# Two gate projections computed in the first stage of a hybrid layer and handed to the second through DRAM, with smaller pools for k, q and scores

## The chip, the cores and the metric

The kernel runs on one core of one Trainium2 chip. The metric is the device time of one execution in microseconds (us). A core has five engines with a queue each: the tensor engine (PE), the vector engine (DVE), the scalar engine (ACT), GpSimd (POOL) and the sync engine (SP), which here issues every transfer. An engine takes its queue strictly in the order in which it was written, so an instruction that waits holds back all behind it.

## The reference, cut to what matters

One layer over 4096 prompt tokens and 8 short sequences of 16 tokens (128 sample tokens), model width 1024:

```python
h = _rmsnorm(x, norm_w)
proj = h @ w_in                                   # one projection, split by columns
qkv, z_a, b_a, a_a, hq, hf, hi, z_b = jnp.split(proj, offs, axis=-1)
qkv_c, new_buf = _causal_conv(qkv, conv_buf, conv_w)
o_a, S_gdn_new = _gated_delta(q_a, k_a, v_a, g, beta, S_gdn, c)      # group A, 8 heads of 64
o_a = _rmsnorm(o_a, gdn_norm_w) * jax.nn.silu(z_a)
o_b, S_hg_new = _hgrn2(q_b, k_b, v_b, logf, S_hg, c)                 # group B, 4 heads of 128
o_b = _rmsnorm(o_b, hg_norm_w) * jax.nn.silu(z_b)
y = x + jnp.concatenate([o_a, o_b], -1) @ w_out   # then a final RMSNorm
```

`z_a` and `z_b` are the two gates, 512 columns each. They depend on x alone and are used only just before the output projection.

## The kernel before

The 33 tiles of 128 tokens form 17 groups: group 0 is the sample tile, groups 1 to 16 have two prompt tiles each. The work runs in two stages.

**Stage A** (`phase_a`) does group A for all groups and leaves its normed output in DRAM (`oa`) and the normed inputs, split in two fp16 parts, in DRAM (`xd`). For a group it projects q, k and v (`proj`: 12 blocks `acc` of 24 matmuls, each followed by ACT, POOL and DVE steps of the convolution, `u`, `c`, `c0`, written to `kq` and `vv`); makes the scores of both tiles (`gdn_pre`: matmuls `pk`, then DVE writes `WA`, lines 573 and 574); sends their diagonal blocks to DRAM (`wdr`) and reads them back spread over the partitions (`N`, line 623); inverts them on DVE by a chain of 62 dependent instructions `tm`, `X` (`gdn_inv`, lines 632 to 639); sends the inverse to DRAM and back (`xdr`, `tx`); transposes it (`tT`, line 656) and couples the blocks (`pv`, `V`, `px`, `tx`). Then the recurrence (`gdn_rec`) runs tile by tile: `pks`, `r`, `py`, `w`, `pcr`, `r`, `pz`, `w`, `pss`, the state `S` (line 737), the output `po`, its norm (`jo`, `no`) and `on` (line 769). The recurrence of a tile is the last reader of its `WA` and of its `kv`, that of a group's second tile the last reader of the group's `kq`.

A program loop with index g has, in this order, the recurrence of group g-1, the scores and the inverse of g, and the projections of g+1. Beside that `wspill` prepares the weights of stage B (`za`, `zb`, `hf`, `hq`, `hi` and the two halves of `w_out`, `o0`, `o1`) in small steps: it splits them in fp16 parts and writes them to DRAM.

**Stage B** (`phase_b`) does group B, gates, output projection and final norm. Per group: `hg_proj` (blocks `hac` of hq and hf), the score levels (`hg_levels`), `hg_tok` (projections `tphi`, `tpza`, `tpzb` of 24 matmuls with 512 columns per tile; the gate as (1 + tanh) times the projection, lines 1039 and 1040) and `hg_tile` (recurrence, norm, gate, output projection `py`, final norm, store). The weights of the gates and of `o0` come from DRAM into the slots in which stage A kept `WA` and `kv`, so they are loaded once A has ended.

Pools decide how far the groups overlap: `WA` and `kv` have 4 buffers (two groups of two tiles), `kq` 3.

The order on each engine is not written out. A scheduler in the framework lays out all instructions once, by the order of the program and its own estimate of the durations and of the free buffers, and each engine then follows that fixed list.

Of the kernel before, what the change touches and what calls it, by code (L numbers as in the profile page):

```python
# [16 lines left out]
P = 128  # L17
# [8 lines left out]
class Kern:  # L26
# [10 lines left out]
    # ---------------------------------------------------------------- consts  # L37
    def consts(self, ctx):
# [15 lines left out]
        # small vectors as rows, transposed on the tensor engine  # L54
# [15 lines left out]
        # conv taps times one half: [p, tap, block]  # L70
# [3 lines left out]
        # -2 exp(A_log), dt_bias on all partitions  # L74
# [7 lines left out]
    def masks(self):  # L82
# [3 lines left out]
        # mi[t, i] = t <= i  # L86
# [3 lines left out]
        # sequence of a token of the sample tile: sm[t, s], b16[t, i], ms[t, i] = b16 and t <= i  # L90
# [23 lines left out]
    def wprep(self, c0, c1, hi, lo, us, stg, eng):  # L114
        """hi + lo = (rows of w_in scaled by norm_w) * s in fp16 parts, us = 1 / (s * XS), s a power of two."""
# [15 lines left out]
    def wspill(self):  # L131
        """the same for the weights of phase B, to DRAM in fp16 parts, by steps of 128 columns"""
# [9 lines left out]
        def stage(nm, src, c):  # L142
            st = self.ex.tile([P, NDC, P], F32, tag="st", name=f"st{nm}{c}")
            with self.tc.issue_after(self.mark.ins):
                nc.sync.dma_start(st, src[:, :, c:c + P])
            nc.gpsimd.tensor_tensor(st, st, fac[nm][:, :, None].to_broadcast([P, NDC, P]), ALU.mult)
            return st

        for nm, src, c0 in names:
            fac[nm] = wrow if src is wout else self.nw  # L150
            self.wd[nm] = self.wdp.tile([P, 2, NDC, 512], F16, tag=f"wd{nm}", name=f"wd{nm}")
# [27 lines left out]
        for nm, src, c0 in names:  # L179
# [11 lines left out]

    def wa(self, name):
        return self.ex.tile([P, 2, 8, P], F32, tag="WA", name=name, bufs=4)
# [6 lines left out]
    # ---------------------------------------------------------------- phase A  # L200
    def shared(self, ctx):
        """what both phases use"""
# [4 lines left out]
        self.qp = pool("qp", 3)  # L207
# [8 lines left out]
    def phase_a(self, oa, xd):  # L216
        nc, tc, i, o = self.nc, self.tc, self.i, self.o
        with ExitStack() as ctx:
# [15 lines left out]
            def stage(g):  # L234
                if g < 4:
# [3 lines left out]
                return self.qp.tile([P, NDC, 256], F32, tag="kq", name="wst5")  # L239
# [7 lines left out]
            # last rows of the sample's convolution state, as columns  # L247
# [25 lines left out]
            # current tap, on the unscaled projection  # L273
# [8 lines left out]

            spill = self.wspill()
            nsp = -(-84 // max(ng - 1, 1))
            for g in range(-1, ng + 1):
# [60 lines left out]
    def xload(self, g, k, d):  # L346
        """x of a tile, normed, times XS"""
        nc = self.nc
        if k == 0:
# [7 lines left out]
        nc.scalar.activation(d["xl"][:, :, k * P:k * P + P], x.rearrange("p (c e) -> p c e", c=NDC), AF.Square,  # L357
                             accum_out=ss[:, 0:1])
        # XS * (mean + eps) ** -0.5
# [4 lines left out]
    def xtrans(self, g, k, d, xd):  # L364
        """its fp16 parts with the channels on the partitions"""
# [20 lines left out]
    def gate(self, g, d):  # L386
        """beta; decays: cumulative G, exp(total - G), G along the free axis in DRAM."""
# [24 lines left out]
        # softplus(y) = max(y, 0) + 2 atanh(e / (2 + e)), e = exp(-|y|)  # L412
# [44 lines left out]
    def mm3(self, out, wh, wl, xh, xl):  # L457
        """out = w^T x over the chunks, without the product of the low parts."""
# [7 lines left out]
    def proj(self, g, d):  # L466
# [7 lines left out]
        if samp:  # L474
            # states of the sequences [r k, s, p, v] for the head pairs p = 0, 1 and 2, 3
            Sn = [kq[:, 1].rearrange("p s (q v) -> p s q v", v=64),
                  self.wa("Sn1")[:, 0].rearrange("p h (a b) -> p h a b", a=2)]
# [39 lines left out]
    def gdn_pre(self, g, k, d):  # L517
# [16 lines left out]
        # exp(G) by channel; decay between tokens of the chunk, [j, h, i], zero for i < j  # L534
# [13 lines left out]
        # token layout of k, q, v  # L548
# [6 lines left out]
        kv = self.ex.tile([P, 2, 8, 64], F32, tag="kv", name=f"kv{nm}", bufs=4)  # L555
# [22 lines left out]
        # its value at the end of the chunk, or of the sequences  # L578
# [5 lines left out]
    def gdn_pre2(self, g, k, d):  # L584
# [10 lines left out]
        # 64 * eps * sum, for the norm of o  # L595
# [5 lines left out]
        # k, q times exp(G)  # L601
# [24 lines left out]
        # rows of the identity, those of one parity on one half of the partitions  # L626
# [13 lines left out]
        # to [j of 64, h, i of 64] by way of DRAM  # L640
# [33 lines left out]
    def gdn_rec(self, g, k, d, oa):  # L674
# [53 lines left out]
        # state  # L728
# [32 lines left out]
        # norm of the heads  # L761
# [11 lines left out]
    def b_begin(self, xd):  # L773
        """weights and first projections of phase B, in the place of those of phase A"""
        nc, w = self.nc, self.wp
        self.B = {}
# [25 lines left out]
        # za, zb, o0 go where A keeps what it needs of a tile  # L802
# [390 lines left out]
```

## Time and profile before

| | us |
|---|---|
| three timed runs | 2981.66, 2983.92, 2987.39 |
| median | 2983.92 |
| profiled execution, span from the first to the last instruction | 2983.5 |

| over the span | PE | DVE | ACT | POOL |
|---|---|---|---|---|
| busy us | 2598.1 | 1752.2 | 1219.2 | 991.0 |
| share | 87% | 59% | 41% | 33% |

The profiled execution's own time is its span, 2983.5 us; it lies 0.4 us from the median, so there is nothing to account for around the span. The shares are means over two stages that are limited differently: stage A lasts to about 1540 us, stage B from there to the end, with some overlap. Busy time of PE counts each matmul from its start to its modelled end, and successive matmuls overlap, so the distance between two starts says how fast PE works. A wait is put down to what ended last.

### The profile page before, as it was taken

Reading aid. Unit: us, or ns where it says so; the run is one execution under the profiler, and the core shown is the slowest. Engines: PE = TensorE matmul, PEld = TensorE weight load, DVE = VectorE, ACT = ScalarE, POOL = GpSimd, SP = SyncE. Lnnn points to the kernel's source line nnn. Section 1 sums busy time; section 2 is a strip of 40 time slices with the busy share of each in tenths; the row PEclk is TensorE's granted clock in tenths of the full one; section 3 lists DMA queues with packets and bytes.
Section 4 is the critical chain, followed back from the end, with each engine's and each line's share of the span. In section 5 each row is a group of like instructions: output and inputs, shape, how many; then the busy total and the mean of one; then the engine's idle time right before and its main releaser. Section 6 shows DMA issues by size and latency. Waiting matters only on the chain.

```text
span 2983.5 us, 67579 instructions
## 1 busy us (share of the span) xinstructions
PE 2598.1 (87%) x27628; PEld 1847.4 (62%) x27628; DVE 1752.2 (59%) x4215; ACT 1219.2 (41%) x3930; POOL 991.0 (33%) x1300
## 2 busy tenths in 40 slices
PE   4768678877877887778899999999999999999997
PEld 4656566665666666666674666666656666665664
DVE  7786778777778788876644434444433344433343
ACT  6656565555555665555332222222222222222222
POOL 5755565465565665655320001110001111000110
PEclk9888999888898989888999999999999999999999
DMA  6334232233343333333233231111110111111010
GB/s 180 100 100 122 68 107 74 73 101 106 98 121 77 96 103 99 97 94 115 77 92 112 73 98 40 43 51 44 51 47 24 46 44 50 44 51 34 32 37 33
DMA packets 298701, 227.78 MB, mean 76 GB/s; under 512 B 186409, under 2 KB 263614, under 8 KB 293782
## 3 DMA queue, kind: packets, MB, share of 16 engines
q1 hardware_dynamic: 298390, 223.45, 25.6%
q8 instruction: 217, 3.56, 0.5%
q14 instruction: 94, 0.77, 0.1%
HBM read 151.78 MB, written 71.62 MB: 75 GB/s over the span
## 4 chain that ended last, share of the span: by engine, by line
PE 49%; DVE 28%; DMA 13%; ACT 2%; issue 2%; POOL 2%; SPq 2%; DVEq 0%; POOLq 0%; ACTq 0%
DMA N<-wdr 7%; DVE X L638 6%; DVE c L510 5%; DVE tm L636 5%; PE py L1016 4%; PE py L1014 4%; PE py L1015 4%; PE hac L462 4%; PE hac L464 4%; PE hac L463 4%; PE sc L954 2%; PE tpzb L1014 2%; PE tpza L1014 2%; PE tpzb L1015 2%; PE tpzb L1016 2%
## 5 line engine op out<-in xcount | busy, mean ns | idle before, releaser
L462 PE MATMUL acc<-xt,w 128*128 128x256 f16 (+1 forms) x1632 | 468.9, 289 | 38.5 <-ACT c L504 36.8
L464 PE MATMUL acc<-xt,w 128*128 128x256 f16 (+1 forms) x1632 | 468.0, 288 | 2.7 <-DVE w L129 2.7
L463 PE MATMUL acc<-xt,w 128*128 128x256 f16 (+1 forms) x1632 | 468.9, 289 | 0.0
L510 DVE SCALAR_TENSOR_TENSOR c<-u,cw,c 128x256 f32<-128x256 f32 (+1 forms) x408 | 237.0, 584 | 31.0 <-POOL c L508 29.8
L1145 DVE SCALAR_TENSOR_TENSOR xr<-py,ysc,xr 128x512 f32<-128x512 f32 x66 | 49.5, 750 | 302.3 <-PE py L1016 302.3
L638 DVE TENSOR_TENSOR X<-X,tm 128x126 f32<-128x126 f32 (+26 forms) x527 | 220.5, 418 | 7.3
L512 ACT ACTIVATE c<-c 128x256 f32<-128x256 f32 (+1 forms) x204 | 83.4, 409 | 322.3 <-DVE c L510 197.6
L463 PEld LDWEIGHTS <-w 128*128 128x128 f16 x1632 | 171.9, 105 | 67.8 <-issue 41.3
L1014 PE MATMUL py<-wo,oh 128*128 128x512 f16 x528 | 201.0, 381 | 4.7 <-ACT oh L1137 3.5
L1016 PE MATMUL py<-wo,ol 128*128 128x512 f16 x528 | 201.1, 381 | 0.2
L1015 PE MATMUL py<-wo,oh 128*128 128x512 f16 x528 | 201.0, 381 | 0.0
L462 PEld LDWEIGHTS <-w 128*128 128x128 f16 x1632 | 172.2, 106 | 37.6 <-issue 9.9
L464 PEld LDWEIGHTS <-w 128*128 128x128 f16 x1632 | 172.0, 105 | 33.5 <-issue 3.3
L636 DVE TENSOR_TENSOR tm<-X,N 128x126 f32<-128x126 f32 (+26 forms) x527 | 187.9, 357 | 7.1
L1048 POOL TENSOR_TENSOR zs<-zs,pw_m 128x1 f32<-128x1 f32 x33 | 20.9, 632 | 469.6 <-DVE zs L1047 469.6
L508 POOL TENSOR_TENSOR c<-c,c 128x256 f32<-128x256 f32 (+1 forms) x204 | 155.9, 766 | 50.9 <-ACT c L507 41.8
L462 PE MATMUL hac<-bxt,whq 128*128 128x256 f16 (+1 forms) x544 | 147.4, 273 | 9.0 <-DVE q L924 9.0
L463 PE MATMUL hac<-bxt,whq 128*128 128x256 f16 (+1 forms) x544 | 147.2, 273 | 0.0
L464 PE MATMUL hac<-bxt,whq 128*128 128x256 f16 (+1 forms) x544 | 147.0, 273 | 0.0
L462 PE MATMUL hac<-bxt,whf 128*128 128x256 f16 (+1 forms) x544 | 145.4, 270 | 0.0
L464 PE MATMUL hac<-bxt,whf 128*128 128x256 f16 (+1 forms) x544 | 145.4, 270 | 0.0
L463 PE MATMUL hac<-bxt,whf 128*128 128x256 f16 (+1 forms) x544 | 145.3, 270 | 0.0
(399 smaller groups left out, 6692.3 us busy)
## 6 DMA issues: line engine op xcount, KB each, us to landing
E<-gdr SPq DMA_DIRECT2D x33, 512.0 KB
out_dram<-xr SPq DMA_DIRECT2D x33, 512.0 KB
x<-in_x_prompt_dram SPq DMA_DIRECT2D x32, 512.0 KB
xd<-xt SPq DMA_DIRECT2D x16, 1024.0 KB
bxt<-xd SPq DMA_DIRECT2D x16, 1024.0 KB
xr<-in_x_prompt_dram SPq DMA_DIRECT2D x32, 512.0 KB
tx<-xdr SPq DMA_DIRECT2D x66, 128.0 KB
oa<-on SPq DMA_DIRECT2D x33, 256.0 KB
```

Of the source, the lines that this page charges most:

```text
L462: nc.tensor.matmul(out, wh[k], xh[k], start=(k == 0), stop=False)
L463: nc.tensor.matmul(out, wh[k], xl[k], start=False, stop=False)
L464: nc.tensor.matmul(out, wl[k], xh[k], start=False, stop=(k == n - 1))
L508: nc.gpsimd.tensor_tensor(c, c, c0, ALU.add)
L510: nc.vector.scalar_tensor_tensor(cv, taps[j], self.cw[:, j, b:b + 1], cv, ALU.mult, ALU.add)
L512: nc.scalar.activation(th, c, AF.Tanh)
L636: nc.vector.tensor_tensor(tv, X[:, 0:R, m:m + 1].to_broadcast([2 * SY, R, c]), N[:, m:m + 1, m + 1:32].to_broadcast([2 * SY, R, c]), ALU.mult)
L638: nc.vector.tensor_tensor(X[:, 0:R, m + 1:32], X[:, 0:R, m + 1:32], tv, ALU.subtract)
L954: nc.tensor.matmul(ps[b:b + 32, k, h], KS[:, k, h, b:b + 32], rhs(k, h, slice(b, b + 32)), start=True, stop=True, tile_position=(0, b))
L1014: nc.tensor.matmul(acc, xh[:, dc], wh[dc], start=(dc == 0), stop=False)
L1015: nc.tensor.matmul(acc, xh[:, dc], wl[dc], start=False, stop=False)
L1016: nc.tensor.matmul(acc, xl[:, dc], wh[dc], start=False, stop=(dc == NDC - 1))
```

## The change

The gates are projected in stage A. `wspill` now prepares `za` and `zb` first and leaves them in on-chip memory. From group 3 on, `zproj` follows `proj` of the same group and writes the finished gate of a tile to DRAM (`zd`) in two halves; for the groups 0 to 2 (5 tiles) it comes after the last group's projections, on inputs that are loaded again (`zload`). Stage B loads the gate (`zg`, 512 KB a tile) in place of the projections. The weights `o0` and `o1` of stage B go where `za` and `zb` were. `WA` and `kv` go from 4 to 3 buffers and `kq` from 3 to 2, and some staging slots of the start change. The temporary `zt` shares the two slots `on` of the recurrence's output and of the weights' fp16 parts.

```diff
-        for nm, src, c0 in names:
+        for nm, src, c0 in names[:2]:
+            yield from sums(nm, src, c0)
+        for nm, src, c0 in names[:2]:
+            t = w.tile([P, 2, NDC, 512], F16, tag=f"w{nm}", name=f"w{nm}")
+            self.B[nm] = [[t[:, e, dc] for dc in range(NDC)] for e in range(2)]
+            for c in range(4):
+                st = stage(nm, src, c0 + c * P)
+                cc = slice(c * P, c * P + P)
+                nc.scalar.copy(t[:, 0, :, cc], st)
+                nc.gpsimd.tensor_tensor(t[:, 1, :, cc], st, t[:, 0, :, cc], ALU.subtract)
+                yield
...
+    def zproj(self, g, d):
+        nc = self.nc
+        for k, t in enumerate(self.groups[g]):
+            for n, name in enumerate(("za", "zb")):
+                acc = self.tokproj(name, d["xh"], d["xl"], k, f"{g}_{k}")
+                zt = self.tp.tile([P, 512], F32, tag="on", name=f"zt{g}_{k}_{n}")
+                nc.scalar.activation(zt, acc, AF.Tanh, scale=self.us5[name])
+                nc.vector.scalar_tensor_tensor(zt, zt, 1.0, acc, ALU.add, ALU.mult)
+                nc.sync.dma_start(self.zd[t][:, 512 * n:512 * n + 512], zt)
+    def zload(self, g, xd):
+        xt = self.xtp.tile([P, 2, NDC, 2 * P], F16, tag="xt", name=f"zxt{g}")
+        N = len(self.groups[g]) * P
+        nc = self.nc
+        if N == 2 * P:
+            nc.sync.dma_start(xt, xd[g])
+        else:
+            nc.sync.dma_start(xt[:, :, :, 0:N], xd[g][:, :, :, 0:N])
+        return {"xh": xt[:, 0, :, 0:N], "xl": xt[:, 1, :, 0:N]}
...
-        return self.ex.tile([P, 2, 8, P], F32, tag="WA", name=name, bufs=4)
+        return self.ex.tile([P, 2, 8, P], F32, tag="WA", name=name, bufs=3)
...
-        self.qp = pool("qp", 3)
+        self.qp = pool("qp", 2)
...
-            nsp = -(-84 // max(ng - 1, 1))
+            nsp = -(-60 // max(ng - 4, 1))
+            late = min(3, ng)
...
                     self.proj(g + 1, st[g + 1])
-                for _ in range(0 if g < 0 else nsp if g < ng - 2 else 99):
+                    if g + 1 >= late:
+                        self.zproj(g + 1, st[g + 1])
+                for _ in range((8, 4, 4)[g + 1] if g < 2 else nsp if g < ng - 2 else 99):
                     next(spill, None)
                 if g == ng - 1:
+                    for z in range(late):
+                        self.zproj(z, self.zload(z, xd))
...
-        kv = self.ex.tile([P, 2, 8, 64], F32, tag="kv", name=f"kv{nm}", bufs=4)
+        kv = self.ex.tile([P, 2, 8, 64], F32, tag="kv", name=f"kv{nm}", bufs=3)
...
-        for n, nm in enumerate(("hf", "hq", "hi")):
-            t = w.tile([P, 2, NDC, 512], F16, tag=f"w{n}", name=f"w{nm}")
+        for nm, tag in (("hf", "w0"), ("hq", "w1"), ("hi", "w2"), ("o0", "wza"), ("o1", "wzb")):
+            t = w.tile([P, 2, NDC, 512], F16, tag=tag, name=f"w{nm}")
...
+        zg2 = self.ex.tile([P, 2, 2, 512], F32, tag="WA", name=f"zg{g}", bufs=3)
         for k, t in enumerate(self.groups[g]):
             nm = f"{g}_{k}"
             v = vs[k]
-            if k == 0:
-                zg2 = self.qp.tile([P, 2, 2, 512], F32, tag="kq", name=f"zg{g}")
             zg = zg2[:, k]
-            for n, name in enumerate(("za", "zb")):
-                acc = self.tokproj(name, xh, xl, k, nm)
-                nc.scalar.activation(zg[:, n], acc, AF.Tanh, scale=self.us5[name])
-                nc.vector.scalar_tensor_tensor(zg[:, n], zg[:, n], 1.0, acc, ALU.add, ALU.mult)
-                if n == 0:
-                    yield
+            nc.sync.dma_start(zg, self.zd[t].rearrange("p (a b) -> p a b", a=2))
```

Since the scheduler orders the engines anew, the diff doesn't show where the work now stands. Three places follow. In these rows a name ends with the group, the tile of the group and a buffer number: `WA9_1_...` are the scores of the second tile of group 9. Line numbers are those of the kernel that the rows belong to; in the changed kernel the lines 616, 617, 699, 756, 766, 780, 812 and 675 are what 573, 574, 656, 713, 723, 737, 769 and 632 were.

DVE in the kernel before, from the transposed inverse of group 8 to the first step on the scores that were read back for group 9:

```order
L656 STREAM_TRANSPOSE tT8_0_10099<-tx8_0_10096 128x256
...
L574 TENSOR_TENSOR WA9_1_11094<-pk9_1_0_11095,E9_11014 128x2x2x128
L766 SCALAR_TENSOR_TENSOR no7_1_9890<-no7_1_9890,nrm7_8799 128x8
...
L769 TENSOR_TENSOR on7_1_9901<-po7_1_9817,no7_1_9890 128x512
L573 TENSOR_TENSOR WA9_1_11094<-pk9_1_1_11102,E9_11014 128x2x2x128
L574 TENSOR_TENSOR WA9_1_11094<-pk9_1_1_11102,E9_11014 128x2x2x128
...
L632 TENSOR_TENSOR N9_11121<-N9_11121,cs9_11122 128x1024
```

The same stretch of DVE in the changed kernel:

```order
L699 STREAM_TRANSPOSE tT8_0_10811<-tx8_0_10808 128x256
...
L756 TENSOR_TENSOR r8_0_11678<-kv8_0_10644,pks8_0_11667 128x512
...
L766 TENSOR_TENSOR r8_0_11678<-r8_0_11678,pcr8_0_11691 64x512
...
L780 TENSOR_TENSOR S_438<-S_438,pss8_0_11711 64x4x64 x2
...
L616 TENSOR_TENSOR WA9_1_11924<-pk9_1_0_11925,E9_11844 128x2x2x128
...
L812 TENSOR_TENSOR on8_0_11750<-po8_0_11666,no8_0_11739 128x512
L616 TENSOR_TENSOR WA9_1_11924<-pk9_1_1_11932,E9_11844 128x2x2x128
L617 TENSOR_TENSOR WA9_1_11924<-pk9_1_1_11932,E9_11844 128x2x2x128
...
L675 TENSOR_TENSOR N9_11951<-N9_11951,cs9_11952 128x1024
```

Before, what stands between the two was the tail of group 7's recurrence; group 8's own (`r8`) stood behind N9. Now the recurrence of group 8's first tile stands ahead of the scores of group 9's second tile, and so ahead of N9.

PE in the changed kernel, from the gates of group 9 to the recurrence of group 8:

```order
L1045 MATMUL tpza9_0_11514<-wza_1846,xt9_9218 128x512
...
L1045 MATMUL tpzb9_0_11543<-wzb_3015,xt9_9218 128x512
...
L1045 MATMUL tpza9_1_11572<-wza_1846,xt9_9218 128x512
...
L1045 MATMUL tpzb9_1_11601<-wzb_3015,xt9_9218 128x512
...
L703 MATMUL pv8_0_10813<-tT8_0_10811,WA8_0_10650 32x32 x16
...
L711 MATMUL px8_1_10877<-tx8_1_10852,V8_1_10874 32x32 x16
...
L728 MATMUL pks8_0_11667<-S_438,kq8_9841 128x128 x4
```

The 96 matmuls of a group's gates now stand as one block ahead of `pv`, the first matmul on the transposed inverse. Between `pv8_0` and `pks8_0` lie 96 `acc` matmuls of group 10.

The queue of SP in the changed kernel, ahead of the load of N9:

```order
L814 DMA oa_93<-on8_0_11750 128x512
L620 DMA wdr9_11843<-WA9_1_11924 32x8x32 x4
L576 DMA E10_13059<-gdr10_12200 128x1024 x2
L666 DMA N9_11951<-wdr9_11843 128x1x1024
```

Before, the store of `on7_1` stood ahead of these `wdr` stores, and no load of `E` between them and the load of N9.

More of the change, by code (lines that the diff above doesn't have):

```diff
@@ L143, in stage @@
             st = self.ex.tile([P, NDC, P], F32, tag="st", name=f"st{nm}{c}")
-            with self.tc.issue_after(self.mark.ins):
+            with self.tc.issue_after(self.mark.ins) if self.mark else ExitStack():
                 nc.sync.dma_start(st, src[:, :, c:c + P])
@@ L147, in stage, with sums @@
             return st
-        for nm, src, c0 in names:
+        def sums(nm, src, c0):
             fac[nm] = wrow if src is wout else self.nw
-            self.wd[nm] = self.wdp.tile([P, 2, NDC, 512], F16, tag=f"wd{nm}", name=f"wd{nm}")
             ssq = w.tile([P, 4], F32, tag=f"ssq{nm}", name=f"ssq{nm}")
@@ L178, in wspill @@
             fac[nm] = f
-        for nm, src, c0 in names:
+        for nm, src, c0 in names[:2]:
[9 more added lines that the diff above has]
+                yield
+        for nm, src, c0 in names[2:]:
+            self.wd[nm] = self.wdp.tile([P, 2, NDC, 512], F16, tag=f"wd{nm}", name=f"wd{nm}")
+            yield from sums(nm, src, c0)
+        for nm, src, c0 in names[2:]:
             for c in range(4):
@@ L234, in stage @@
             def stage(g):
-                if g < 4:
+                if g < 3:
                     return self.wa(f"wst{g}").rearrange("p a b c -> p (a b c)").rearrange("p (d c) -> p d c", d=NDC)
@@ L238, in stage @@
                     return self.ex.tile([P, NDC, 256], F32, tag="E", name="wst4")
-                return self.qp.tile([P, NDC, 256], F32, tag="kq", name="wst5")
+                return self.qp.tile([P, NDC, 256], F32, tag="kq", name=f"wst{g}")
             z = self.ex.tile([P, 520], F32, tag="N", name="z")
@@ L476, in proj @@
             Sn = [kq[:, 1].rearrange("p s (q v) -> p s q v", v=64),
-                  self.wa("Sn1")[:, 0].rearrange("p h (a b) -> p h a b", a=2)]
+                  self.ex.tile([P, 8, P], F32, tag="kv", name="Sn1", bufs=3).rearrange("p h (a b) -> p h a b", a=2)]
             sv = self.i["state_gdn"][0].rearrange("s (q r) k v -> r k s q v", r=2)
@@ L801, in b_begin @@
             pass
-        for nm, tag, c in (("za", "WA", 4), ("zb", "WA", 4), ("o0", "kv", 2)):
-            self.B[nm] = [[], []]
-            for c0 in range(0, NDC, c):
-                t = self.ex.tile([P, 2, c, 512], F16, tag=tag, name=f"w{nm}{c0}", bufs=4)
-                nc.sync.dma_start(t, self.wd[nm][:, :, c0:c0 + c])
-                for e in range(2):
-                    self.B[nm][e] += [t[:, e, dc] for dc in range(c)]
     def phase_b(self, oa, xd):
@@ L820, in phase_b @@
             w = self.w
-            t = w.tile([P, 2, NDC, 512], F16, tag="wo1", name="wo1")
-            nc.sync.dma_start(t, self.wd["o1"])
-            self.B["o1"] = [[t[:, e, dc] for dc in range(NDC)] for e in range(2)]
             self.epsq = w.tile([P, 1], F32, tag="epsq", name="epsq")
@@ L1161, in build @@
         oa = dr.tile([npt + 1, P, 512], F32, tag="oa", name="oa")
+        k.zd = dr.tile([npt + 1, P, D], F32, tag="zd", name="zd")
         xd = dr.tile([k.ng, P, 2, NDC, 2 * P], F16, tag="xd", name="xd")
```

8 lines of the change are left out of this document (4 added, 4 removed).

## The prediction

> **What bounds the kernel now.** First the page, for the share of each engine and its course over the span.
>
> ```profile
> span 2983.5 us, 67579 instructions
> PE 2598.1 (87%) x27628; PEld 1847.4 (62%) x27628; DVE 1752.2 (59%) x4215; ACT 1219.2 (41%) x3930; POOL 991.0 (33%) x1300
> PE   4768678877877887778899999999999999999997
> DVE  7786778777778788876644434444433344433343
> PEclk9888999888898989888999999999999999999999
> ```
>
> The rows of 40 slices show two regimes: up to slice 20 (about 1500 us) DVE leads and PE has gaps, behind it PE is full. Two stretches, one from each stage, then DVE's waits in stage A:
>
> ```profile
> 1800.00:2678.00 878.00, 878.00 (x8945) 549.55 (x8943) 352.02 (x796) 211.98 (x515) 85.07 (x110) 1.00 0.13 43
> 600.00:1370.00 770.00, 602.35 (x6693) 490.04 (x6692) 609.30 (x1450) 443.44 (x1621) 451.53 (x580) 0.89 0.36 99
> DVE N L632 <- DMA N<-wdr: 156.6, 15, 13.3
> DVE tT L656 <- DMA tx<-xdr: 44.5, 23, 4.2
> 178.56 1.88 DVE L632 TENSOR_TENSOR N<-N,cs 128x1024 f32<-128x1024 f32 x1 [9.75 <-DMA cs<-cdr]
> L632 DVE TENSOR_TENSOR N<-N,cs x17: 1218/1225/1883, 106.3 to 1461.6; 128x1024 f32<-128x1024 f32 x16, 64x1024 f32<-64x1024 f32 x1
> ```
>
> The columns of a stretch are its length and the busy time of PE, PEld, DVE, ACT and POOL, the granted clock, the DMA share and GB/s. Stage B is bound by PE: 878 busy of 878 us, DVE 40%. Stage A is bound by DVE with its waits: 609 of 770 busy (79%), and the largest wait is one per group, about 10 us in the mean and 13.3 at most, for N. The first N, the sample group's, is at 106.3, that of group 1 at 178.6, the 17th at 1461.6: 15 turns of 85.5 us.
>
> The chain of waits around one turn of stage A, groups 7 and 8 (start, us, what):
>
> ```profile
> 702.15 1.23 DVE N L632
> ...
> 740.21 0.69 DVE r L713
> ...
> 750.02 0.68 DVE X L639
> ...
> 753.33 2.20 DMA xdr<-X
> ...
> 757.60 3.10 DMA tx<-xdr
> 760.80 0.45 DVE tT L656
> ...
> 767.46 1.61 POOL no L767
> 769.10 0.69 DVE on L769
> 769.79 0.60 DVE WA L573
> 770.38 0.61 DVE WA L574
> ...
> 772.61 2.95 DMA wdr<-WA
> 775.58 13.52 DMA N<-wdr
> 789.12 1.23 DVE N L632
> ```
>
> Read it as two phases. From N to the end of X, 702.15 to 750.7, 48.6 us: the elimination, with the next group's convolution and the last group's recurrence filling DVE between its steps. From there to the next N, 38.4 us: 10.1 to tT, 10.2 until the last WA is written, 18.1 for the way of the scores through DRAM. The first `r` of a second tile's recurrence stands at 740.2, ahead of X's end: the recurrence runs under the elimination of the next group. That needs a group's scores while the last group's are still held, which four buffers allow.
>
> **The change part by part.** *Stage B loses the gates' projections.* Their rate is read from starts, since busy times overlap:
>
> ```profile
> 2400.73 0.38 PE L1014 MATMUL tpzb<-wzb,bxt 128*128 128x512 f16 x1
> ...
> 2405.70 0.38 PE L1016 MATMUL tpzb<-wzb,bxt 128*128 128x512 f16 x1
> 1424.63 0.27 PE L463 MATMUL acc<-xt,w 128*128 128x256 f16 x1
> 1424.74 0.27 PE L464 MATMUL acc<-xt,w 128*128 128x256 f16 x1
> ```
>
> From the first to the 24th of a block are 23 steps, 4.97 us: 0.216 us each, 5.19 a block. 33 tiles with two blocks: 342 us off a PE that is full. ACT's and DVE's part (0.69 us each a block) leaves with them and lay under PE. The load of the finished gate takes their place, 33 times 512 KB, ahead of its use, with DMA 13% busy: nothing, unless it comes late.
>
> *The gates come back in stage A.* A group's 96 matmuls are 20.7 us of PE. Their place in the new order, a block ahead of `pv`, falls in the second half of the elimination, when PE has little to do. I take nothing for them: after the last `acc` PE must wait for X's end and the 10.1 us to tT. If that cover were gone, 20.7 us a group. DVE and ACT get four instructions a group, DVE 4 x 0.688 = 2.75 us, and SP four stores at 0.33 us of issue, by these rows (the store is of the same kind):
>
> ```profile
> L1040 DVE SCALAR_TENSOR_TENSOR zg<-zg,tpza 128x512 f32<-128x512 f32 x33 | 22.7, 688 | 46.5 <-ACT zg L1039 46.5
> L1039 ACT ACTIVATE zg<-tpza,u5za 128x512 f32<-128x512 f32 x33 | 22.6, 686 | 97.1 <-PE tpza L1016 91.6 <-PE po L687 5.4
> 661.81 0.33 SPq L771 DMA_DIRECT2D oa<-on  x1
> ```
>
> *Three buffers for WA and kv, two for kq.* This is the part that I expect to decide. Two buffers hold group g, the third the first tile of g+1; the second tile's scores must wait until the recurrence of g's first tile has read its own for the last time. The new order shows just that: `r8_0`, `S` and `on8_0` stand ahead of the last `WA9_1`, and so of N9. What ran under the elimination becomes a link between two eliminations: X, tT, coupling, recurrence, WA, wdr, N, X. Its pieces, from rows:
>
> ```profile
> 664.52 0.69 DVE L723 TENSOR_TENSOR r<-r,pcr 64x512 f32<-64x512 f32 x1
> 665.26 1.14 PE L726 MATMUL pz<-r,tx 64*64 64x64 f32 x16
> ...
> 682.14 0.69 DVE L769 TENSOR_TENSOR on<-po,no 128x512 f32<-128x512 f32 x1 [0.70 <-POOL no L767]
> L719 ACT COPY w<-py 64x512 f32<-64x512 f32 x33 | 18.9, 572 | 8.3 <-PE py L718 8.1
> L765 ACT ACTIVATE jo<-po 128x64 f16<-128x64 f32 x264 | 59.5, 225 | 24.9 <-PE po L759 20.6
> L765 ACT ACTIVATION_READ_ACCUMULATOR jo<-po 128x1 f32 x264 | 53.5, 203 | 0.0
> L767 POOL TENSOR_TENSOR no<-no,pw_m 128x8 f32<-128x8 f32 x33 | 55.8, 1690 | 44.8 <-DVE no L766 32.6 <-DMA out_dram<-S 11.6
> ```
>
> (1) X's end to tT: 10 us as now. (2) tT to `pks`: 96 `acc`, 0.11 us apart by the two `acc` rows above, are 10.6 us, with `pv`, `px` and transposes some 15; bare, 3. (3) `pks` to the second `r`: py and pcr like pz 1.14 each, w 0.57, r twice 0.69, pks about 1: 5.2 to 7. (4) Second `r` to the end of `on`: 18.3 us as measured (664.52 to 682.83, part of it DVE waiting for tT); bare, pz, w, pss, po 3.6, eight squares 8 x 0.43 = 3.4, the power 1.69, two r-sized steps: 10.5. I take 14. (5) the last WA, two of 0.6: 1.2. (6) wdr to N: 18.1 as measured, and the two issues for E that now stand ahead of it, 1. Sum 10 + 15 + 6 + 14 + 1.2 + 19 = 65 us where 38.4 stood; bare 10 + 3 + 5.2 + 10.5 + 1.2 + 18.1 = 48; with (2) to (4) held up as far as today's worst rows, 71.
>
> Queued behind these waits: on DVE the convolution of group g+2 from its third block, since two buffers for kq hold its target until `r` of the second tile has gone; on SP the N load stands behind `on`'s store. So DVE has only about 20 us of other work in the 65.
>
> From N to X's end I keep 48: 3 us of work moved into the wait, 2.75 came, the recurrence's stalls left. A turn is 48 + 65 = 113, bare 48 + 48 = 96, worst 119. Turns in which more of the convolution stands in the wait (the first, and three later ones) come out shorter; I take 110 in the mean.
>
> [...]
>
> *The ends.* Before the first full turn, 16 weight steps of the gates now precede group 3, each with a POOL step of about 1.9 us; eight of them ahead of the first scores. Bounds 0 and 16, I take 10.
>
> ```profile
> L146 POOL TENSOR_TENSOR stza<-stza,cols 128x1024 f32<-128x1024 f32 x4 | 7.7, 1931 | 1.8 <-DMA stza<-in_w_in_dram 1.7
> 1424.70:1461.60 36.90, 17.41 (x144) 0.00 (x0) 2.36 (x5) 1.00 0.45 137
> ```
>
> From N of group 16 (1461.6) to the end are 1521.9 us now, PE nearly full. Off go 342. On come the late gates of groups 1 and 2, 41 (those of group 0 fit into the wait before), and stage B's first projections, which the second row (tile `hac`, the 36.9 us before 1461.6, PE's 144 matmuls) shows running earlier now: 144 x 0.11 = 16. The recurrence of group 15, then done already, takes off 13 (two tiles, pks, py, pcr, pz, pss and po, some 6.5 us of PE each). 1521.9 - 342 + 41 + 16 - 13 = 1224.
>
> **Sum against the profiled execution's own 2983.5** (the median 2983.92 lies 0.4 off): the 15 turns take 85.5 each now. At 110: 2983.5 + 10 + 15 x (110 - 85.5) - 298 = 2983.5 + 10 + 367.5 - 298 = 3063 us. The break-even lies at (298 - 10) / 15 = 19.2 us more a turn, 104.7.
>
> **The rivals.** *The link is short (faster).* Place: (2) to (4), `pv` to `on`. If PE and ACT reach the coupling and the recurrence nearly bare because their queues are empty in the wait, a turn is 96 to 102: 2983.5 + 10 + 15 x (10.5 to 16.5) - 298 = 2853 to 2943. For it: ACT is 58% busy in stage A. Against it: 96 `acc` stand ahead of `pks` in PE's fixed order, and the 18.3 of the row above was measured in just such a wait.
>
> *Nothing becomes serial (much faster).* If the turn stayed at 85.5 plus 2.75, stage A swallows the gates: 2983.5 + 10 + 41 - 298 = 2737. PE's slack speaks for it, the order of `r8_0` ahead of N9 against it. A smaller matter here is the clock: the granted clock is 0.89 in stage A and 1.00 in B, so a PE kept busy could do the some 20 us of (2) and (3) a tenth faster, 15 x 2 = 30 us in all, and a PE left idle longer could lose as much; the range holds both. [...]
>
> *The link is longer (slower still).* The gates and the weights' fp16 parts share two slots with `on`, and their stores stand in SP's queue ahead of wdr; each that is late delays N. From 119 a turn: 2983.5 + 10 + 15 x 33.5 - 298 = 3198 and more.
>
> *Stage B doesn't give the 342 back.* If the gate's load came late or the levels lost their cover, B keeps part; at half, 171 more. The new order fills the levels with the next group's `hac`, so this only widens the top.
>
> **How the numbers follow.** Forecast, a turn of 103 to 117 (2958 to 3168): 0.67. Short link: 0.16. Nothing serial: 0.05. Longer, or B stays: 0.12. This kernel's measurement can tell 0.2%, 6 us, from no change. Slower: nearly all of the forecast's case but what lies under 104.7 a turn, and the last: 0.73. Same 0.03, faster 0.24. Time 3063; the forecast's own range is 2958 to 3168; over the cases I give 2890 to 3180.
>
> **What would show it.** Right: N of neighbouring groups 105 to 117 us apart; from X's end to N some 65, the recurrence of g's first tile wholly within it; DVE's idle time in a turn more than doubled from 18 us, put down to N, `pks`, `pcr` and `on`; stage B 20.7 us shorter for two tiles, with PE full. Wrong: turns under 100, `pks` within 5 us of tT, or gaps of PE in B.

## The result and the profile after

The changed kernel takes 3048.5 us (median of 4 runs, 3047.4 to 3050.9) against 2983.6 of the kernel before on the same chip: the ratio is 1.022, with a 95% interval of 1.020 to 1.023. It is slower. The profiled execution spans 3049.2 us, 65.7 more than the profiled one of before.

The page of the changed kernel, its head and three rows of the 40 slices:

```profile
span 3049.2 us, 68002 instructions
PE 2662.1 (87%) x27628; PEld 1895.2 (62%) x27628; DVE 1678.3 (55%) x4215; ACT 1228.9 (40%) x3930; POOL 987.3 (32%) x1300
PE   4668778779888897898789879998999999999996
DVE  7776755664675557555636543534444454444443
PEclk8878899899988998999889989999999999999998
```

The two regimes are there again, but the border has moved from slice 20 to slice 24, some 1830 us. In the first stage DVE has fallen from sevens and eights to mostly fives to sevens, and PE has risen to mostly sevens to nines. The second stage is shorter and PE is still full there. The same stretches as before (length, busy time of PE, PEld, DVE, ACT and POOL, granted clock, DMA share, GB/s):

```profile
1900.00:2800.00 900.00, 882.09 (x10375) 602.04 (x10364) 421.72 (x988) 243.95 (x631) 110.82 (x146) 0.99 0.24 79
600.00:1370.00 770.00, 662.40 (x6363) 486.69 (x6362) 457.64 (x1206) 383.24 (x1360) 347.55 (x463) 0.90 0.29 83
```

In the second row DVE is busy 59% of the time where it was 79%. Nothing in the first stage is near its limit but PE with 86%, and that is not what ends a turn, as the rows of one turn show. First the times of N, then turn 7 on DVE, on PE (the first and the last of the group's 96 gate matmuls, and `pks`), and the last transfer from the chain of waits:

```profile
L675 DVE TENSOR_TENSOR N<-N,cs x17: 1218/1226/1226, 107.3 to 1793.8; 128x1024 f32<-128x1024 f32 x16, 64x1024 f32<-64x1024 f32 x1
```
```profile
196.75 1.23 DVE L675 TENSOR_TENSOR N<-N,cs 128x1024 f32<-128x1024 f32 x1 [7.79 <-DMA N<-wdr]
...
864.49 1.23 DVE L675 TENSOR_TENSOR N<-N,cs 128x1024 f32<-128x1024 f32 x1 [9.04 <-DMA N<-wdr]
...
911.15 0.69 DVE L682 TENSOR_TENSOR X<-X,cs 128x512 f32<-128x512 f32 x1
...
921.17 0.45 DVE L699 STREAM_TRANSPOSE tT<-tx 128x256 f32<-128x256 f32 x1 [8.45 <-DMA tx<-xdr]
...
939.66 0.68 DVE L756 TENSOR_TENSOR r<-kv,pks 128x512 f32<-128x512 f32 x1
...
943.54 0.69 DVE L766 TENSOR_TENSOR r<-r,pcr 64x512 f32<-64x512 f32 x1 [2.60 <-PE pcr L765]
...
953.69 0.68 DVE L617 TENSOR_TENSOR WA<-pk,E 128x512 f32<-128x512 f32 x1
...
954.78 0.69 DVE L812 TENSOR_TENSOR on<-po,no 128x512 f32<-128x512 f32 x1 [0.41 <-POOL no L810]
...
975.63 1.23 DVE L675 TENSOR_TENSOR N<-N,cs 128x1024 f32<-128x1024 f32 x1 [5.49 <-DMA N<-wdr]
```
```profile
900.01 0.38 PE L1045 MATMUL tpza<-wza,xt 128*128 128x512 f16 x1
...
922.74 0.38 PE L1047 MATMUL tpzb<-wzb,xt 128*128 128x512 f16 x1
...
936.56 0.61 PE L728 MATMUL pks<-S,kq 128*128 128x128 f32 x4
```
```profile
958.25 17.36 DMA N<-wdr
```

From N of group 1 to the 17th N there are 15 turns, 196.75 to 1793.8: 106.5 us each, where it was 85.5. In turn 7 the end of X, 911.8, is followed by 63.8 us in which everything comes one after another: tT, the first `r`, the second `r`, the last WA, `on`, the way through DRAM, N. The recurrence of the group's first tile (939.7 to 955.5) lies wholly between two eliminations. The gates' matmuls fill PE from 900.0 to 923.1, that is the end of the elimination and the wait for tT.

Where the 65.7 us come from, in the two profiled executions: N of group 1 is 18.2 later (178.56 to 196.75); the 15 turns take 15 x 21.0 = 314.0 more; from the 17th N to the end it is 1255.4 where it was 1521.9, 266.5 less. 18.2 + 314.0 - 266.5 = 65.7.

### The profile page after: what moved, and what is told of

The parts are those of the page before. It is cut to its first block, busy times and chain, and to the rows that moved or that the text cites. A ratio compares the mean times of both kernels' runs of the same rounds, so it can differ in the third digit from the quotient of the medians.

```text
span 3049.2 us, 68002 instructions
## 1 busy us (share of the span) xinstructions
PE 2662.1 (87%) x27628; PEld 1895.2 (62%) x27628; DVE 1678.3 (55%) x4215; ACT 1228.9 (40%) x3930; POOL 987.3 (32%) x1300
## 4 chain that ended last, share of the span: by engine, by line
PE 53%; DVE 19%; DMA 15%; ACT 4%; issue 4%; POOL 3%; SPq 2%; POOLq 0%; DVEq 0%; ACTq 0%
DMA N<-wdr 6%; PE py L1045 4%; PE py L1047 4%; PE py L1046 4%; PE hac L505 4%; PE hac L506 3%; PE hac L507 3%; DVE tm L679 3%; DVE X L681 3%; DVE c L553 3%; PE sc L985 2%; PE tphi L1045 2%; PE tphi L1046 2%; DMA x<-in_x_prompt_dram 2%; PE tphi L1047 2%
## 5 line engine op out<-in xcount | busy, mean ns | idle before, releaser
L553 DVE SCALAR_TENSOR_TENSOR c<-u,cw,c 128x256 f32<-128x256 f32 (+1 forms) x408 | 225.0, 557 | 63.3 <-POOL c L551 61.5
L679 DVE TENSOR_TENSOR tm<-X,N 128x126 f32<-128x126 f32 (+26 forms) x527 | 174.6, 331 | 8.6
L681 DVE TENSOR_TENSOR X<-X,tm 128x126 f32<-128x126 f32 (+26 forms) x527 | 169.1, 321 | 8.7
L1174 POOL TENSOR_TENSOR ys<-ys,pw_m 128x1 f32<-128x1 f32 x33 | 19.9, 603 | 416.0 <-DVE ys L1173 416.0
L505 PE MATMUL hac<-bxt,whq 128*128 128x256 f16 (+1 forms) x544 | 145.3, 270 | 4.4 <-DVE q L955 4.4
L1172 ACT ACTIVATE oh<-xr 128x1024 f16<-128x1024 f32 x33 | 34.9, 1056 | 281.5 <-DVE xr L1170 268.6
L506 PE MATMUL hac<-bxt,whq 128*128 128x256 f16 (+1 forms) x544 | 145.1, 269 | 0.0
```

What stands on the lines that cost most here:

```text
L505: nc.tensor.matmul(out, wh[k], xh[k], start=(k == 0), stop=False)
L506: nc.tensor.matmul(out, wh[k], xl[k], start=False, stop=False)
L553: nc.vector.scalar_tensor_tensor(cv, taps[j], self.cw[:, j, b:b + 1], cv, ALU.mult, ALU.add)
L679: nc.vector.tensor_tensor(tv, X[:, 0:R, m:m + 1].to_broadcast([2 * SY, R, c]), N[:, m:m + 1, m + 1:32].to_broadcast([2 * SY, R, c]), ALU.mult)
L681: nc.vector.tensor_tensor(X[:, 0:R, m + 1:32], X[:, 0:R, m + 1:32], tv, ALU.subtract)
```

## The experiments

All were timed beside the kernel before; "turn" is the mean of the 15 from N of group 1 to the 17th N. An edit also makes the scheduler lay out every engine anew, so no run differs from another in its edit alone: the run with WA 3, kv 3, kq 3 below has one buffer more than that with kq 2 and is still 18 us slower. The turns in the expectations were read from a mark of N's wait, which in some turns lies up to 9 us ahead of N itself. So they name 105.9 for the changed kernel and 101.9 for the one with few buffers, where N's own rows give 106.5 and 102.6. For the same reason they name a start of 21 us and 257 us behind N16 instead of 18.2 and 266.5. The numbers below are N's own.

The theory of the prediction: fewer buffers of WA and kv make the recurrence of a group's first tile a link between two eliminations, and the gates' matmuls lie under waits. The rival: the buffers matter little, and the gates' own work in the first stage lengthens the turn. The first four runs take the two halves of the change apart.

**The buffers alone.**

```
 before, and:
-  tag="WA", bufs=4 / tag="kv", bufs=4 / pool("qp", 3)
+  tag="WA", bufs=3 / tag="kv", bufs=3 / pool("qp", 2)
   (za, zb, o0 and the gates' tile get other places in the second stage)
```

> The kernel before with three buffers for WA, three for kv and two for kq, and nothing else of the change: the gates' projections stay in the second stage (their weights only get other places there). Theory (the buffers make the recurrence of a group's first tile a link between two eliminations): N's 100 to 106 us apart instead of 85.7, from X's end to N 55 to 62 us instead of 33; in all 2983.5 + 15 x (103 - 85.7) - 13 = 3230 us, 3170 to 3290. Rival (the gates' own matmuls, evictions, slots and stores in the first stage lengthen the turn, the buffers hardly): turn below 90, time at most 3050.

```profile
L632 DVE TENSOR_TENSOR N<-N,cs x17: 1219/1225/1227, 96.5 to 1718.2; 128x1024 f32<-128x1024 f32 x16, 64x1024 f32<-64x1024 f32 x1
```
```profile
179.04 1.23 DVE L632 TENSOR_TENSOR N<-N,cs 128x1024 f32<-128x1024 f32 x1 [11.26 <-DMA N<-wdr]
...
856.15 0.69 DVE L639 TENSOR_TENSOR X<-X,cs 128x512 f32<-128x512 f32 x1
...
866.46 0.45 DVE L656 STREAM_TRANSPOSE tT<-tx 128x256 f32<-128x256 f32 x1 [2.95 <-DMA tx<-xdr]
...
877.84 0.69 DVE L713 TENSOR_TENSOR r<-kv,pks 128x512 f32<-128x512 f32 x1 [1.10 <-PE pks L685]
...
894.02 0.69 DVE L769 TENSOR_TENSOR on<-po,no 128x512 f32<-128x512 f32 x1 [1.73 <-POOL no L767]
...
895.23 0.68 DVE L574 TENSOR_TENSOR WA<-pk,E 128x512 f32<-128x512 f32 x1
...
913.38 1.23 DVE L632 TENSOR_TENSOR N<-N,cs 128x1024 f32<-128x1024 f32 x1 [11.96 <-DMA N<-wdr]
```

3221.6 us, ratio 1.079 (1.078 to 1.081). Turn (1718.2 - 179.0) / 15 = 102.6, X's end to N 58.7. The buffers alone cost 17.1 us a turn, which is the theory's number; the rival's "hardly" is refuted. The rows of its turn 7 show the link without any gates: behind the end of X come tT, the recurrence of the group's first tile (`r` to `on`), the last WA and then N.

**Which buffers.** The same edit, once with three for kq and once with only kq lowered.

```
 e2: WA 3, kv 3, kq 3          e3: WA 4, kv 4, kq 2
```

> The kernel before with three buffers for WA and kv and three for kq as before; the gates stay in the second stage. Theory (WA and kv decide, kq does not): turn 98 to 104, time 3170 to 3260. Rival (two buffers of kq, which hold back the convolution of the group after next, are what lengthens the turn): turn 86 to 90, time at most 3050.

> The kernel before with four buffers for WA and kv as before and two for kq; the gates stay in the second stage. Theory (WA and kv decide): turn 86 to 90, time 2980 to 3050. Rival (kq decides): turn 100 or more, time 3190 or more.

Three of WA and kv with three of kq: 3240.0 us (1.086, 1.084 to 1.088), turn 103.3, as the theory had it. Four of WA and kv with two of kq: 3095.2 us (1.037, 1.036 to 1.039), turn 94.1. That lies between the two expectations: kq alone costs 8.6 us a turn, so the theory's 86 to 90 was too low. But beside three of WA and kv the third kq gives nothing back (103.3 against 102.6). WA and kv decide; with four of each, kq alone costs half as much. Whether WA or kv is the one that decides was not tested: both were lowered together.

**The gates alone.**

```
 after, and:
-  tag="WA", bufs=3 / tag="kv", bufs=3 / pool("qp", 2)
+  tag="WA", bufs=4 / tag="kv", bufs=4 / pool("qp", 3)
-  t = w.tile([P, 2, NDC, 512], F16, tag=f"w{nm}")     # za and zb, two parts each
+  t = w.tile([P, NDC, 512], F16, tag="wz")            # one tile for all four
   (o0 and o1 get other places in the second stage)
```

> The changed kernel with the buffers of before (four, four, three): the gates' projections are in the first stage with all their matmuls, evictions and stores. To make room both gates multiply by one and the same 8 KB tile of weights a partition, twice, in place of their own two parts: the work is the same, the gates' values are not the reference's. Theory (the buffers are the loss): turn 87 to 93; with the changed kernel's start of 21 us and its gain of 257 behind N16, 2983.5 + 21 + 15 x (1.5 to 7.5) - 257 = 2770 to 2860. Rival (the gates' own work lengthens the turn): turn 100 or more, 2963 or more.

```profile
L676 DVE TENSOR_TENSOR N<-N,cs x17: 1217/1226/1226, 116.0 to 1689.0; 128x1024 f32<-128x1024 f32 x16, 64x1024 f32<-64x1024 f32 x1
```
```profile
193.61 1.23 DVE L676 TENSOR_TENSOR N<-N,cs 128x1024 f32<-128x1024 f32 x1 [9.60 <-DMA cs<-cdr]
...
847.25 0.69 DVE L683 TENSOR_TENSOR X<-X,cs 128x512 f32<-128x512 f32 x1
856.84 0.45 DVE L700 STREAM_TRANSPOSE tT<-tx 128x256 f32<-128x256 f32 x1 [5.19 <-DMA tx<-xdr]
...
878.69 0.68 DVE L618 TENSOR_TENSOR WA<-pk,E 128x512 f32<-128x512 f32 x1
...
898.87 1.22 DVE L676 TENSOR_TENSOR N<-N,cs 128x1024 f32<-128x1024 f32 x1 [6.84 <-DMA N<-wdr]
```

2974.8 us, ratio 0.997 (0.995 to 0.998). Turn (1689.0 - 193.6) / 15 = 99.7: the theory's 87 to 93 fell. The gates alone cost 14.2 us a turn, nearly as much as the buffers alone, and the two together not 31.3 but 21.0. The rows show how. In the mean of the turns the last WA, the scores of the next group, is written 26.5 us after the first tT (here 856.84 to 879.4, 22.5); in the kernel before it was 10.2. The last matmuls of the scores (`pk`) stand behind the gates' 21 us in PE's fixed order. With few buffers the scores are late anyway, held back by the recurrence, and the same block lies under that wait.

**Is it the matmuls or what hangs on them?** Three of the 24 matmuls of a block are left; its eviction by ACT and DVE, its slots and its store stay.

```
-  acc = self.tokproj(name, d["xh"], d["xl"], k, ...)   # 24 matmuls
+  three matmuls, of the first of eight chunks
```

> The run with the gates in the first stage and four, four and three buffers, with 3 of the 24 matmuls of each gate block left (one of the eight chunks, so the gates' values are not the reference's); evictions, slots and stores stay. That run's turn was 99.7 us. Theory (PE's room: a turn of before leaves PE 85.7 x (1 - 602/770) = 18.7 us idle and the gates' matmuls need 20.7, so they stand ahead of the next group's scores): turn 85 to 89; less 15 x (11 to 15) and 45 of the late gates from 2975: 2705 to 2765. Rival (what delays is the blocks' evictions on ACT and DVE, their slots and stores): turn 96 or more, 2875 or more.

> The changed kernel, its buffers as they are, with 3 of the 24 matmuls of each gate block left (gates' values not the reference's). Its turn is 105.9, that of the kernel before with the same few buffers 101.9. Theory (the 4 us between them are the gates' matmuls on PE): turn 100 to 103, 3048.5 - 15 x (3 to 6) - 45 = 2914 to 2958. Rival (evictions, slots and stores): turn 105 or more, 2990 or more.

With the buffers of before: 2781.1 us (0.932, 0.930 to 0.934), turn 89.0. With the change's buffers: 2983.1 us (0.9995, 0.998 to 1.001), turn 103.5. The 84 matmuls a group that are gone are 10.7 of the 14.2 us in the one case and 3.0 of the 3.9 in the other; the 12 that are left, evictions, slots and stores are the rest. The turns came out near the theory: 89.0 is the upper end of 85 to 89, and 103.5 lies just above 100 to 103, with 3.0 us less than the change where 3 to 6 were named. Both times missed: 2705 to 2765 and 2914 to 2958 were named. They took off 45 us for the late gates, and behind the 17th N only 31 and 19 us went (1282.1 to 1251.1; 1255.4 to 1236.1). The late gates lie in part beside the last group's elimination.

**Half of the gates.** Only `za` is computed in the first stage, `zb` stays in the second. Half the resident weights leave room for all buffers.

```
-  for n, name in enumerate(("za", "zb")):  acc = self.tokproj(...)   # first stage
+  for n, name in enumerate(("za",)):       acc = self.tokproj(...)
   second stage:
+  nc.sync.dma_start(zg[:, 0], self.zd[t])
+  acc = self.tokproj("zb", xh, xl, k, nm)   # and its tanh and product, as before
   (newc in the place of sc, hro in that of cro, the rows' square in that of xl, as room for the buffers)
```

> The reference's computation in full: only the first half of the gates (za) is computed in the first stage and goes through DRAM, zb stays in the second stage; so half the resident weights, and four, four and three buffers as before. Theory (PE's room): 10.4 us of gates in 18.7 us of room, turn 86 to 90; start +9, behind N16 about half of 240 less: 2983.5 + 9 + 15 x (0.5 to 4.5) - 120 = 2880 to 2940. Rival (a block ahead of the scores costs its share whatever room PE has; half of the 14 us that both halves cost): turn 92 to 94, 2965 to 3000.

2955.6 us, ratio 0.991 (0.989 to 0.992). Turn 91.4, X's end to N 45.4, the last WA 17.8 us after tT. Neither expectation holds: the turn lies between them, and the time below the rival's and above the theory's. Room on PE (10.4 us of gates in 18.6 idle) did not make the half free. With four, four and three buffers the turn rises with one measure, how late the scores come after tT: 10.2 and 85.5 (before), 14.3 and 89.0 (thin), 17.8 and 91.4 (half), 26.5 and 99.7 (all). Of 16.3 us that the scores come later, 14.2 arrive in the turn. That measure is itself a piece of the turn, so it says where the time stands; that it stands there because of the gates' place in PE's order is read from the rows, and the next run puts it to a test.

**Another place.** In the run with all gates and all buffers, a group's gates are issued behind its own scores and the start of its elimination.

```
-  self.proj(g + 1, ...); self.zproj(g + 1, ...)
+  self.gdn_inv(g, ...);  self.zproj(g, ...)       # one iteration later
   (the slot of x's transpose is taken in xtrans instead of xload)
```

> The run with both gates in the first stage, one common 8 KB tile of weights (the gates' values not the reference's) and four, four and three buffers, with one move: a group's gates are issued one iteration later, behind its own scores and the start of its elimination, instead of ahead of them; x's slot is therefore held until then. Its turn was 99.7. Theory A (what costs is that the block stands ahead of the scores): behind them PE has the wait for N, so turn 88 to 92, 2975 - 15 x (8 to 12) = 2795 to 2855. Theory B (the amount costs: 20.7 us have to go somewhere, and the order now lets the next projections wait for x's slot and the recurrence stand ahead of N again): turn 98 to 108, 2950 to 3100.

```profile
PE tpza L1055 <- DVE zt L216: 133.1, 12, 17.6
PE acc L508 <- ACT c L550: 51.5, 35, 10.0
```

3134.7 us, ratio 1.051 (1.049 to 1.053), turn 110.1. Theory A fell, and the turn is even above B's range. PE's longest waits (in total, times, longest) point to why: the gates now wait on PE for the eviction of the gates before them, 133 us in twelve waits, and the next projections, the convolution and the scores stand behind: the last WA comes 52.9 us after tT. The same matmuls cost 24.6 us a turn here and 14.2 ahead of the scores, so the place matters; but the later claim of x's slot came with the move, and its share was not taken apart. A place for 20.7 us that costs nothing was not found.

**Half of the gates, weights earlier.** With the half kernel, all eight weight steps of `za` come ahead of the first scores, so that one tile's gates are late instead of five.

```
-  late = min(3, ng)          /  steps (4, 2, 2), then 6 a turn
+  late = min(1, ng)          /  steps 8, then 5 a turn
```

> The half kernel (za in the first stage, zb in the second, four, four and three buffers; the reference's computation in full) with all eight weight steps of za ahead of the first group's scores instead of four, so that only the sample group's za comes late, one tile instead of five. Expected if the late gates are what stands behind N16: start +6 to +10, behind N16 20 to 35 less, turn as it was (88 to 92): 2925 to 2950. If they are hidden there anyway (with thin gates only 14 us went of 45): start +6 to +10 and behind N16 at most 10 less: 2950 to 2965.

2933.6 us, ratio 0.984 (0.981 to 0.986): the fastest run here that computes the gates in full (the thin one, 2781.1, doesn't), and faster than both kernels. The time lies in the first range, but by other terms than named: the start is 33.6 us later than in the half kernel (N of group 1 at 216.1 against 182.6, not 6 to 10), the turn 90.8, and behind the 17th N it is 46.6 less (1353.0 against 1399.6, not 20 to 35). The four tiles' `za` are 4 x 5.19 = 20.8 us of matmuls, less than half of the 46.6; what else left, and why the start costs so much, was not taken apart.

| kernel | turn | X's end to N | last WA after tT | N of group 1 | behind the 17th N | time |
|---|---|---|---|---|---|---|
| before | 85.5 | 36.8 | 10.2 | 178.6 | 1521.9 | 2983.6 |
| the change | 106.5 | 66.0 | 38.3 | 196.7 | 1255.4 | 3048.5 |
| buffers alone | 102.6 | 58.7 | 31.1 | 179.0 | 1501.7 | 3221.6 |
| gates alone | 99.7 | 52.8 | 26.5 | 193.6 | 1282.1 | 2974.8 |
| gates alone, thin | 89.0 | 40.5 | 14.3 | 195.6 | 1251.1 | 2781.1 |
| the change, thin gates | 103.5 | 59.2 | 30.4 | 198.2 | 1236.1 | 2983.1 |
| half of the gates | 91.4 | 45.4 | 17.8 | 182.6 | 1399.6 | 2955.6 |
| half, weights earlier | 90.8 | 45.7 | 17.9 | 216.1 | 1353.0 | 2933.6 |
| WA 3, kv 3, kq 3 | 103.3 | 59.0 | 30.3 | 182.2 | 1505.5 | 3240.0 |
| WA 4, kv 4, kq 2 | 94.1 | 51.0 | 24.0 | 178.4 | 1503.6 | 3095.2 |
| gates alone, moved | 110.1 | 79.0 | 52.9 | 194.7 | 1283.6 | 3134.7 |

## Why the prediction was right, point by point

**The sign and the cause.** Forecast 3063, measured 3048.5, within the forecast's own 2958 to 3168. By the terms of the sum: start +8.2, turns -53.5, behind the 17th N +31.5, which leads from 3063 to the profiled 3049.2; so the time is nearer than its terms, whose errors partly cancel; that part of the nearness is luck. The mechanism is the one named: the recurrence of the first tile became a link, and the run with the buffers alone shows it without any of the rest.

**The link, 65 us.** Measured 66.0 in the mean. By its pieces: X to tT 9.2 (10 named), tT to `pks` 17.3 (15), `pks` to the second `r` 8.4 (6), to the end of `on` 12.3 (14), last WA 0.3 (1.2), from there to N 18.5 (19; 17.4 of it are the load of N in turn 7, which in the row of before took 13.5). The sum held better than its parts. But the second and the third contain the gates: with the buffers alone they are 10.2 and 7.8, and the gap is 58.7. The prediction saw the `acc` matmuls of the next group between `pv` and `pks`, and from turn 3 to 14 there are 57 to 96 of them; with the buffers alone, and with thin gates, there are none. So some 7 us of the link are matmuls that stand behind tT only with the gates' block ahead of them; they belong to the gates, not to the buffers, and the shorter elimination gives 3.4 of them back.

**From N to X's end, "I keep 48".** This is the term of the turn that was mis-sized. It measured 40.5 (43.9 with the buffers alone; 48.8 in the mean of before). More than the 3 us of work taken out left the elimination. So a turn is 66.0 + 40.5 = 106.5 where 65 + 48 = 113 was summed. The 110 for the mean came nearer, but not for its reason: the first turn was to be among the shorter ones, and it is the longest, 120.2, with the next three at 118.6, 112.7 and 110.3. Over 15 turns it is 314 instead of 367.5, 53 us of the forecast.

**"I take nothing" for the gates' matmuls.** Right in this kernel to 3 us a turn: the block ends at 923.1, 2 us behind tT. Its cover was named (the wait from X's end to tT), and the price without the cover, 20.7, was not reached in any run with the block ahead of the scores: the gates alone cost 10.7 for the matmuls and 3.5 for the rest, but there half of the block still lies ahead of tT (in the mean from 11.5 us before it to 11.1 behind it). And the cover is the link itself, which the prediction did not say: the two costs take each other's place, 17.1 and 14.2 apart, 21.0 together.

**The ends.** The start measured 18.2, with bounds 0 and 16 and 10 taken: outside. Behind the 17th N, -266.5 where -298 was summed. Counted to the first group's last level in the second stage, which ACT's copy marks at 1545.5 before and at 1921.7 after, the tail took 44.0 us more, and 41 + 16 - 13 is 44. That the sum meets it so closely is in part luck: with thin gates 45 us of late matmuls are gone, and this tail is only 22.9 shorter (105.0 instead of 127.9). What failed is the 342: from that mark to the end only 310 went. The turn with the sample group holds 23 of the missing 32, the rows of before and of after:

```profile
1648.60:1806.10 157.50, 153.96 (x1566) 105.00 (x1564) 62.35 (x143) 39.71 (x97) 14.09 (x21) 1.00 0.27 89
DVE hSn L1105 <- DMA hSn<-in_state_hgrn_dram: 23.5, 4, 7.3
```
```profile
1980.60:2130.00 149.40, 136.63 (x1390) 96.41 (x1388) 58.22 (x131) 35.17 (x85) 15.57 (x22) 0.98 0.34 109
DVE hSn L1130 <- DMA hSn<-in_state_hgrn_dram: 18.4, 4, 6.8
```

Three tiles' gates, 31 us, leave it, and it becomes only 8.1 shorter. PE was full there (154.0 of 157.5) and is not now (136.6 of 149.4): it idles 12.8 us instead of 3.5, which is 9.2 of the 23. DVE waits four times for the states' transfers, 18.4 us, but before it did so for 23.5, so these waits are not new; that the gates' matmuls filled PE beside them is likely but not shown. The other 14 us were not followed; beside the gates the two stretches don't hold quite the same matmuls (120 of `tphi` where there were 72, 384 of `hac` where there were 462). "PE nearly full" was taken for the whole stage from a stretch that lay behind this turn. Elsewhere two tiles became 19.4 us shorter (87.65 to 68.3), with 20.7 named, and PE stayed full. The gate's load never showed.

**The rivals.** *Short link*, 96 to 102 a turn: no; PE did not run bare. *Nothing serial*, 2737: not this kernel, and the run with the gates alone shows that even with all buffers the time would have been 2975, since the order places the gates ahead of the scores. The thin run, 2781, comes nearest to it, with seven eighths of the gates' matmuls left out. *Longer link*, 119 or more: no. *The second stage keeps part*: yes, 32 of 342.

**What was to show it.** N's apart 105 to 117: in the mean 106.5. The gap some 65: 66.0. DVE idle in a turn more than doubled from 18: 106.5 x (1 - 457.6/770) = 43. But it is spread over many waits; the one for N became smaller, not larger. The first row is from before, the others from the changed kernel:

```profile
DVE N L632 <- DMA N<-wdr: 91.3, 9, 13.0
DVE tT L699 <- DMA tx<-xdr: 61.8, 15, 8.5
DVE N L675 <- DMA N<-wdr: 59.8, 7, 11.2
DVE xss L403 <- ACT xj L401: 32.7, 10, 6.8
```

The last three are DVE's longest waits from 600 to 1370 us now. N is 8.5 us a wait, where it was 10.1 in the same stretch before. Who looks only at the longest wait would have found nothing wrong in the changed kernel.

## What to carry to other kernels

A buffer count is a statement on what may overlap: count how many groups' tiles must be alive for two links of the chain to lie beside each other, and look in the new order whether the later group's first step has moved behind the earlier group's last. A block of matmuls that "fits into an idle engine" can still cost when it stands ahead of what the chain needs next in that engine's fixed order: here half of the gates, 10.4 us in 18.6 idle, lengthened the turn by 5.9. Its share of the busy time doesn't tell what it costs. When a change has two costs, measure each alone and both: here 17.1 and 14.2 us apart were 21.0 together, so repairing one alone gives back little: 3.9 us a turn when the gates go, 6.8 when the buffers come back.

## What was not expected of the hardware

In the first stage the granted clock was lower in the kernels in which PE was busy less of the time. Over the eleven profiled kernels, from 600 to 1370 us, it was 0.78 to 0.81 where PE was busy 71 to 77% of the time, 0.87 to 0.89 at 78 to 80%, and 0.90 to 0.92 at 85 to 87%. Three of them, the buffers alone, the change with thin gates, and the gates alone:

```profile
600.00:1370.00 770.00, 554.70 (x5579) 455.80 (x5574) 499.67 (x1262) 374.82 (x1358) 395.97 (x498) 0.80 0.30 85
```
```profile
600.00:1370.00 770.00, 589.81 (x5771) 480.88 (x5771) 475.79 (x1265) 391.89 (x1383) 365.52 (x477) 0.78 0.30 85
```
```profile
600.00:1370.00 770.00, 670.98 (x6560) 492.25 (x6555) 503.52 (x1316) 398.47 (x1404) 363.62 (x490) 0.92 0.30 87
```

The clock was 0.89 before (PE 78% busy) and 0.90 with the whole change (86%); here it is 0.80 (72%), 0.78 (77%) and 0.92 (87%). Which of the two sets the other can't be read from these rows alone, since slower matmuls also keep PE busy longer (0.63 us each instead of 0.38 in the last rows below). With the buffers alone, the same matmuls as before, PE is busy 554.7/770 x 102.6 = 73.9 us a turn instead of 602.35/770 x 85.5 = 66.9. With thin gates in the changed kernel 18 us of matmuls a turn (84 x 0.216) are gone, and PE's busy time fell only from 91.6 to 79.3 (the stretch doesn't hold whole turns, so these are rough; over ten whole turns, from N of group 4 to N of group 14, it is 89.7 and 78.6). So with the buffers alone PE was idle 28.7 us a turn instead of 18.6 and ran under 0.80 instead of 0.89, and with thin gates the 18 us taken out gave back only 11 to 12; how much of the 17.1 us a turn the lower clock makes was not separated. In the changed kernel itself, the clock was neither the gain nor the loss that the prediction weighed: 0.90 for 0.89. One place shows the slow clock at work, PE's rows of the changed kernel behind the 17th N's wait:

```profile
1799.40 2.05 PE L730 MATMUL po<-S,kq 128*128 128x128 f32 x8 [13.41 <-DVE on L812]
1801.24 0.63 PE L1045 MATMUL tpza<-wza,zxt 128*128 128x512 f16 x1
1801.67 0.63 PE L1046 MATMUL tpza<-wza,zxt 128*128 128x512 f16 x1
...
1803.51 0.38 PE L1045 MATMUL tpza<-wza,zxt 128*128 128x512 f16 x1
1803.73 0.38 PE L1046 MATMUL tpza<-wza,zxt 128*128 128x512 f16 x1
```

After 13.4 us without work the matmuls start 0.43 us apart, under a granted clock of 0.50 (1799.4 to 1803.1). From 1803.5 on, 4 us after PE took up work, they start 0.22 apart, under 1.00 (1803.5 to 1812).
